# Choosing the experts of a PEER layer: a shorter list of candidates, one comparison a half, products on another engine

## The chip, the core and the metric

The kernel runs on one core of a Trainium2 chip. The metric is the device time of one execution in microseconds. TensorE (PE) multiplies matrices, VectorE (DVE), ScalarE (ACT) and GpSimd (POOL) work on tiles of 128 partitions, SyncE (SP) issues most of the transfers. Each engine takes its instructions in a fixed order and waits at an instruction until what it needs is there.

## The reference

The program is one decoder layer: two kinds of token mixing side by side, an output projection, and then a feed-forward layer of experts (PEER) for 512 tokens of width 2048. Only the choice of the experts changes. Cut to it, the reference is:

```python
q = (xb @ w_query).reshape(PEER_BLOCK, PEER_HEADS, 2, PEER_HALF)          # 8 heads, 2 halves of 128
s = jnp.einsum('lhpd,hpnd->lhpn', q, sub_keys)                            # 128 scores a half
s_half, i_half = lax.top_k(s, PEER_TOPK)                                  # the best 16 of each half
cand_s = s_half[:, :, 0, :, None] + s_half[:, :, 1, None, :]              # 16 x 16 sums
cand_i = i_half[:, :, 0, :, None] * PEER_N_KEYS + i_half[:, :, 1, None, :]
top_s, pos = lax.top_k(cand_s, PEER_TOPK)                                 # the best 16 sums
eidx = jnp.take_along_axis(cand_i, pos, axis=-1)                          # the experts' numbers
gates = jax.nn.softmax(top_s, axis=-1)
```

Each token so gets 16 of 16384 experts for each of 8 heads. Both lists of 16 are sorted, so the sum of place a in the first and place b in the second can be among the best 16 only if (a+1)(b+1) is at most 16. That holds for 50 pairs.

## The kernel before

The 512 tokens stand as four groups of 128 (`tt`). The stage around the change is the query stage, about 1378 to 1632 us of the span. It is a loop over 8 heads (`h`) and 2 halves (`hf`). For each half a projection `query` runs on TensorE: 16 steps over the width, each with six matmuls (three products of high and low parts, for the first 320 tokens and for the other 192), 96 in all, into a PSUM tile `mm`. The weights come in two pieces a half; `load_split` loads a piece `wr`, ScalarE casts it to its high part `whi`, GpSimd computes the low part `wlo` (helper `split`, lines 201 and 202). There are three `whi` and `wlo` buffers, so a split waits until TensorE has used the piece three before it. ScalarE copies the projection to `qT`, and four score products (L1039) write `sc`, of which there are two buffers. On VectorE follow, for each group of 128 tokens, two rounds of finding the best 8 of 128 with their places (L1043 to L1048).

After both halves of a head VectorE adds the sums into `cand`, 16 rows of 16 a token of which 50 places are used and the rest stays at a very small number (L1056, seven instructions), and finds the best 16 of the 256 places (L1063 to L1068). The position is taken apart into a row and a column (L1073 to L1077). For each half the index is fetched from the list `si` by comparing the place with 0 to 15, multiplying by the list and summing over 16 (`oh`, L1080 and L1082, four instructions each, one for each group of tokens; L1084). The softmax runs between them; its exponential `ex` is on ScalarE (L1088).

After the eighth head TensorE transposes the index tables `iall` and `jall` (L1108), VectorE makes the experts' numbers `ef`, `eu` and `eT`, and the stage of the experts begins: 192 of the tokens gather their own experts by indirect transfers from GpSimd's queue (L1252), and for the other 320 a dense pass over all experts runs on TensorE (`expert_u`, `expert_v`), masked by gates that `gate_block` builds. The first matmuls of that pass (of `expert_u`, also into `mm`) stand in TensorE's order already behind the last query and before the transposes. GpSimd computes `wlo` and `vlo` for the pass.

A scheduler sets each engine's order when the program is built, from the order of the code and its own estimate of durations. The order is fixed in the program. Buffers in a pool with `bufs=n` are used in turn.

## Time and profile before

| | us |
|---|---|
| median of 3 runs | 3998.52 (3996.01 to 4006.34) |
| the profiled execution | 4000.34 |
| its span, first to last instruction | 3998.3 |
| TensorE busy | 3671.5 (92%) |
| VectorE busy | 2473.4 (62%) |
| GpSimd busy | 2385.3 (60%) |
| ScalarE busy | 1455.9 (36%) |

Busy shares are means over stages with different limits. The stage of the change takes about 250 us of the span and is read from slices of its own. Where instructions of one engine follow each other closely, a row's length reaches a little into the next one's start, so the sum of lengths is larger than the time between the first and the last start. A merged row (x4) gives the time from the start of its first to the end of its last. A wait is put down to the event that came last.

### The profile page before, as it was taken

To read this page: it belongs to the slowest core of one execution; us is meant where nothing else is said; L and a number is where in the kernel's file an instruction comes from. 1 tells how busy PE (TensorE), PEld (TensorE's weight loads), DVE (VectorE), ACT (ScalarE), POOL (GpSimd) and SP (SyncE) were. 2 spreads that over 40 slices of the span, in tenths; PEclk is the share of its full clock that TensorE was granted. 3 is DMA by queue.
4 is the path that set the end of the run, shared out by engine and by line. 5 is a ranking of instruction groups with operands and counts; after the bars stand their busy time and mean duration, and the time that the engine had idled before them with its cause. 6 is when DMAs were issued, how large, how long until landed. Compare 5 with 4: busy or idle time off the path is not lost. (4 is left out here: it accounts for less than half of the span.)

```text
span 3998.3 us, 62039 instructions
## 1 busy us (share of the span) xinstructions
PE 3671.5 (92%) x23708; PEld 3046.1 (76%) x23708; DVE 2473.4 (62%) x4503; ACT 1455.9 (36%) x2548; POOL 2385.3 (60%) x1377
## 2 busy tenths in 40 slices
PE   5899999999999899688979999998999999999998
PEld 3667757666656799588858888887888888788888
DVE  7543145455641799898768787566756756674225
ACT  3434323343322411455643333333333333333333
POOL 5345434332413633566637788777878887787765
PEclk9999999998987999899979999999999999999999
DMA  8465662324252422687879988898999989889874
GB/s 338 168 206 176 212 175 72 84 73 132 80 188 79 137 66 77 239 321 281 309 262 338 343 334 331 317 329 317 333 327 344 331 316 328 317 333 337 297 274 127
DMA packets 314008, 964.35 MB, mean 241 GB/s; under 512 B 67376, under 2 KB 132656, under 8 KB 257584
## 3 DMA queue, kind: packets, MB, share of 16 engines
q1 hardware_dynamic: 258416, 557.72, 41.5%
q0 software_dynamic: 55296, 402.68, 26.6%
q8 instruction: 187, 3.06, 0.3%
q14 instruction: 109, 0.89, 0.1%
HBM read 914.34 MB, written 45.94 MB: 240 GB/s over the span
## 5 line engine op out<-in xcount | busy, mean ns | idle before, releaser
L202 POOL TENSOR_TENSOR wlo<-wr,whi 128x1024 fp32r<-128x1024 f32 (+3 forms) x544 | 1048.9, 1936 | 890.6 <-ACT whi L201 810.3
L202 POOL TENSOR_TENSOR vlo<-vr,vhi 128x1024 fp32r<-128x1024 f32 x256 | 633.2, 2482 | 265.9 <-ACT vhi L201 261.3
L207 PE MATMUL mm<-n2hi,wlo 128*128 128x320 f32 x2304 | 733.5, 319 | 39.0 <-POOL wlo L202 38.8
L205 PE MATMUL mm<-n2hi,whi 128*128 128x320 f32 x2304 | 732.5, 318 | 10.8 <-ACT whi L201 7.2
L206 PE MATMUL mm<-n2lo,whi 128*128 128x320 f32 x2304 | 722.4, 314 | 1.9 <-DVE n2lo L202 1.9
L1259 DVE SCALAR_TENSOR_TENSOR g<-g,row 128x1024 f32<-128x1024 f32 x384 | 708.4, 1881 | 3.3 <-DMA g<-in_u,eix 3.3
L201 ACT CAST whi<-wr 128x1024 fp32r<-128x1024 f32 (+3 forms) x544 | 454.3, 841 | 622.4 <-PE mm L206 309.1
L205 PE MATMUL po<-ghi,vhi 128*128 128x320 f32 x2048 | 641.3, 318 | 33.8 <-DVE hT L1224 20.7
L206 PE MATMUL po<-glo,vhi 128*128 128x320 f32 x2048 | 638.9, 314 | 10.4 <-DVE glo L202 10.0
L207 PE MATMUL po<-ghi,vlo 128*128 128x320 f32 x2048 | 616.3, 318 | 22.7 <-POOL vlo L202 22.3
L207 PEld LDWEIGHTS mm<-n2hi,wlo 128*128 128x128 f32 x2304 | 438.7, 190 | 99.4 <-POOL wlo L202 68.7
L205 PEld LDWEIGHTS mm<-n2hi,whi 128*128 128x128 f32 x2304 | 439.7, 191 | 36.4 <-issue 20.8
L205 PEld LDWEIGHTS po<-ghi,vhi 128*128 128x128 f32 x2048 | 391.4, 192 | 83.5 <-DVE hT L1224 24.0
L206 PEld LDWEIGHTS mm<-n2lo,whi 128*128 128x128 f32 x2304 | 439.6, 191 | 5.7 <-issue 3.4
L1184 DVE TENSOR_TENSOR act<-gd,act 128x320 f32<-128x320 f32 x128 | 179.1, 1409 | 418.9 <-ACT act L1158 396.9
L207 PEld LDWEIGHTS po<-ghi,vlo 128*128 128x128 f32 x2048 | 382.2, 192 | 72.0 <-POOL vlo L202 49.0
L1224 DVE SCALAR_TENSOR_TENSOR hT<-po,mod,hT 128x320 f32<-128x320 f32 x512 | 258.6, 544 | 244.3 <-PE po L207 235.2
L206 PEld LDWEIGHTS po<-glo,vhi 128*128 128x128 f32 x2048 | 393.1, 192 | 16.5 <-DVE glo L202 12.2
L201 ACT CAST vhi<-vr 128x1024 fp32r<-128x1024 f32 x256 | 267.8, 1048 | 277.9 <-PE po L206 130.0
L1252 POOL DMA_INDIRECT g<-in_u,eix x192 | 242.1, 1261 | 91.8 <-issue 47.2
L1252 POOL DMA_INDIRECT g<-in_v,eT x192 | 221.7, 1155 | 77.4 <-issue 29.5
L205 PE MATMUL mm<-nhi,whi 128*128 128x512 f32 x640 | 262.7, 410 | 4.5 <-ACT whi L201 4.5
(440 smaller groups left out, 5905.6 us busy)
## 6 DMA issues: line engine op xcount, KB each, us to landing
wr<-in_uT SPq DMA_DIRECT2D x256, 512.0 KB
vr<-in_vq SPq DMA_DIRECT2D x256, 512.0 KB
wr<-in_wrest SPq DMA_DIRECT2D x160, 256.0 KB
aw<-in_ada SPq DMA_DIRECT2D x32, 1024.0 KB
a2w<-in_adar SPq DMA_DIRECT2D x64, 512.0 KB
glD<-gb SPq DMA_DIRECT2D x10, 2048.0 KB
gd<-glD SPq DMA_DIRECT2D x32, 640.0 KB
a3w<-in_adar SPq DMA_DIRECT2D x32, 512.0 KB
```

What stands on the lines that cost most here:

```text
L201: copied.append(S.copy(hi, src))
L202: return (eng or V).tensor_tensor(lo, src, hi.bitcast(F32), OP.subtract)
L205: TE.matmul(ps, lhsT=whi, rhs=xhi, start=first, stop=False)
L206: TE.matmul(ps, lhsT=whi, rhs=xlo, start=False, stop=False)
L207: done_mm[0] = TE.matmul(ps, lhsT=wlo, rhs=xhi, start=False, stop=last)
L1184: V.tensor_tensor(a.rearrange("p (b t) -> p b t", t=TB), gd[:, :, i, :], a.rearrange("p (b t) -> p b t", t=TB), OP.mult)
L1224: V.scalar_tensor_tensor(h, po[d], mod2[:, 48 + k:49 + k], h, OP.mult, OP.add)
L1252: G.indirect_dma_start(out=g, out_offset=None, in_=I[s[0]], in_offset=bass.IndirectOffsetOnAxis(ap=ix, axis=0))
L1259: V.scalar_tensor_tensor(g[:, c], g[:, c], 1.0, n2s[i][:, c], OP.mult, OP.mult, accum_out=wtp[:, e, n:n + 1])
```

## The change

The 50 pairs now stand in ten rows of eight, 80 places a token: the first row holds the sums of place 0 with places 0 to 7 of the other half, the second place 0 with places 8 to 15, rows 2 to 8 the places 1 to 7 with as many as they need, and row 9 the sums of places 8 to 15 of the first half with place 0 of the second. The table has two buffers where it had one. The two rounds of search run over 80 columns. The position needs more steps to become two places (nine instructions on 64 columns in place of four). The comparison is one instruction a half for all four groups of tokens; the product with the index list is one instruction a half too, and moves to GpSimd; `oh` has two buffers. The sum over 16 stays on VectorE. Lines behind the change stand four further down (L1084 is now L1088, L1088 is L1092, L1108 is L1112).

```diff
--- before.py
+++ after.py
@@ -1018,8 +1018,10 @@
         gall = qp.tile([P, 4, P], F32, name="gall", bufs=1)
         iall = qp.tile([P, 4, P], F32, name="iall", bufs=1)
         jall = qp.tile([P, 4, P], F32, name="jall", bufs=1)
-        cand = [qp.tile([P, 4, 16, 16], F32, name="cand", bufs=1)] * 2
-        for t in cand[:1]:
+
+
+        cand = [qp.tile([P, 4, 10, 8], F32, name=f"cand{i}", bufs=1) for i in range(2)]
+        for t in cand:
             V.memset(t, -3.0e38)
         pss = [pu.tile([P, T], F32, name="mm", tag="mm") for _ in range(2)]
         query(pss, 0)
@@ -1049,38 +1051,40 @@
                 V.tensor_copy(si[:, hf], ix)
 
             cd = cand[h % 2]
-            a = 0
-            while a < 16:
-                nb = 16 // (a + 1)
-                e = max(x for x in range(a, 16) if 16 // (x + 1) == nb) + 1
-                V.tensor_tensor(cd[:, :, a:e, 0:nb], sv[:, 0, :, a:e].unsqueeze(3).to_broadcast([P, 4, e - a, nb]),
-                                sv[:, 1, :, 0:nb].unsqueeze(2).to_broadcast([P, 4, e - a, nb]), OP.add)
-                a = e
+            for r0, r1, a0, b0, nb in ((0, 1, 0, 0, 8), (1, 2, 0, 8, 8), (2, 3, 1, 0, 8), (3, 4, 2, 0, 5), (4, 5, 3, 0, 4),
+                                       (5, 6, 4, 0, 3), (6, 9, 5, 0, 2)):
+                V.tensor_tensor(cd[:, :, r0:r1, 0:nb],
+                                sv[:, 0, :, a0:a0 + r1 - r0].unsqueeze(3).to_broadcast([P, 4, r1 - r0, nb]),
+                                sv[:, 1, :, b0:b0 + nb].unsqueeze(2).to_broadcast([P, 4, r1 - r0, nb]), OP.add)
+            V.tensor_tensor(cd[:, :, 9, :], sv[:, 0, :, 8:16], sv[:, 1, :, 0:1].to_broadcast([P, 4, 8]), OP.add)
             tv = qp.tile([P, 4, 16], F32, name="tv")
             px = qp.tile([P, 4, 16], U32, name="px")
             for tt in range(4):
                 c2 = cd[:, tt].rearrange("p a b -> p (a b)")
                 V.max(tv[:, tt, 0:8], c2)
                 V.max_index(px[:, tt, 0:8], tv[:, tt, 0:8], c2)
-                s2_ = qp.tile([P, 256], F32, name="s3")
+                s2_ = qp.tile([P, 80], F32, name="s3")
                 V.match_replace(s2_, tv[:, tt, 0:8], c2, -3.0e38)
                 V.max(tv[:, tt, 8:16], s2_)
                 V.max_index(px[:, tt, 8:16], tv[:, tt, 8:16], s2_)
 
-            for hf, dst in ((0, iall), (1, jall)):
-                pi = qp.tile([P, 4, 16], U32, name="pi")
-                if hf == 0:
-                    V.tensor_scalar(pi, px, 4, None, OP.logical_shift_right)
-                else:
-                    V.tensor_scalar(pi, px, 15, None, OP.bitwise_and)
-                pf = qp.tile([P, 4, 16], F32, name="pf")
-                V.tensor_copy(pf, pi)
-                oh = qp.tile([P, 4, 16, 16], F32, name="oh", bufs=1)
-                for tt in range(4):
-                    V.tensor_tensor(oh[:, tt], pf[:, tt].unsqueeze(2).to_broadcast([P, 16, 16]),
-                                    iota16.unsqueeze(1).to_broadcast([P, 16, 16]), OP.is_equal)
-                    V.tensor_tensor(oh[:, tt], oh[:, tt], si[:, hf, tt].unsqueeze(1).to_broadcast([P, 16, 16]),
-                                    OP.mult)
+            pi = qp.tile([P, 4, 16], U32, name="pi")
+            row, c_ = (qp.tile([P, 4, 16], F32, name=n) for n in ("prow", "pcol"))
+            V.tensor_scalar(pi, px, 3, None, OP.logical_shift_right)
+            V.tensor_copy(row, pi)
+            V.scalar_tensor_tensor(c_, row, -8.0, px, OP.mult, OP.add)
+            ra, rb_ = (qp.tile([P, 4, 16], F32, name=n) for n in ("pa", "pb"))
+            V.scalar_tensor_tensor(ra, row, 9.0, c_, OP.is_equal, OP.mult)
+            V.tensor_tensor(rb_, c_, ra, OP.subtract)
+            V.tensor_scalar(c_, row, 1.0, 8.0, OP.is_equal, OP.mult)
+            V.tensor_tensor(rb_, rb_, c_, OP.add)
+            V.tensor_scalar(row, row, 1.0, -1.0, OP.max, OP.add)
+            V.tensor_tensor(ra, ra, row, OP.add)
+            for hf, r_, dst in ((0, ra, iall), (1, rb_, jall)):
+                oh = qp.tile([P, 4, 16, 16], F32, name="oh", bufs=2)
+                V.tensor_tensor(oh, r_.unsqueeze(3).to_broadcast([P, 4, 16, 16]),
+                                iota16.unsqueeze(1).unsqueeze(1).to_broadcast([P, 4, 16, 16]), OP.is_equal)
+                G.tensor_tensor(oh, oh, si[:, hf].unsqueeze(2).to_broadcast([P, 4, 16, 16]), OP.mult)
                 V.tensor_reduce(dst[:, :, 16 * h:16 * h + 16], oh, mybir.AxisListType.X, OP.add)
 
             ex = qp.tile([P, 4, 16], F32, name="ex")
```

The order moves at three places that matter. The first is GpSimd's queue in the middle of the stage. Before, there are only splits `wlo` of query pieces, four a head; the five rows here are the second piece of head 1, second half, both pieces of head 2, first half, and of head 2, second half:

```order
L202 TENSOR_TENSOR wlo_12340<-wr_12337,whi_12339 128x1024
L202 TENSOR_TENSOR wlo_12498<-wr_12495,whi_12497 128x1024
L202 TENSOR_TENSOR wlo_12552<-wr_12549,whi_12551 128x1024
L202 TENSOR_TENSOR wlo_12640<-wr_12637,whi_12639 128x1024
L202 TENSOR_TENSOR wlo_12694<-wr_12691,whi_12693 128x1024
```

After the change:

```order
L202 TENSOR_TENSOR wlo_12337<-wr_12334,whi_12336 128x1024
L202 TENSOR_TENSOR wlo_12490<-wr_12487,whi_12489 128x1024
L1087 TENSOR_TENSOR oh_12120<-oh_12120,si_12005 128x1024
L1087 TENSOR_TENSOR oh_12124<-oh_12124,si_12005 128x1024
L202 TENSOR_TENSOR wlo_12544<-wr_12541,whi_12543 128x1024
L202 TENSOR_TENSOR wlo_12632<-wr_12629,whi_12631 128x1024
L202 TENSOR_TENSOR wlo_12686<-wr_12683,whi_12685 128x1024
```

The two products of head 0 (`oh`) stand between the two pieces of the first half of head 2 (`wlo_12490` and `wlo_12544`), and so on for each head: the splits behind them wait with them.

The second place is VectorE's queue at the end of a head and the beginning of the next. Before, comparisons, products and sums of head 1 (`oh_12461`, `oh_12475`) are spread among the searches for head 2 (`sv_12492`):

```order
L1080 TENSOR_TENSOR oh_12461<-pf_12459,iota16_11777 128x256 x4
L1091 RECIPROCAL sm_12488<-sm_12488 128x4
L1044 MAX_INDEX ix_12610<-sv_12492,sc_12605 128x8
L1046 MATCH_REPLACE s2_12613<-sv_12492,sc_12605 128x128
L1043 MAX sv_12492<-sc_12605 128x8
L1082 TENSOR_TENSOR oh_12461<-oh_12461,si_12139 128x256 x4
L1092 TENSOR_TENSOR gall_11779<-ex_12485,sm_12488 128x4x16
L1047 MAX sv_12492<-s2_12613 128x8
L1044 MAX_INDEX ix_12610<-sv_12492,sc_12605 128x8
L1046 MATCH_REPLACE s2_12619<-sv_12492,sc_12605 128x128
L1043 MAX sv_12492<-sc_12605 128x8
L1084 TENSOR_REDUCE iall_11780<-oh_12461 128x4x16
```

After the change both comparisons of head 1 come first, and its first sum stands behind ten instructions of the next head's searches:

```order
L1085 TENSOR_TENSOR oh_12469<-pa_12461,iota16_11777 128x1024
L1085 TENSOR_TENSOR oh_12473<-pb_12462,iota16_11777 128x1024
L1045 MAX sv_12484<-sc_12597 128x8
L1046 MAX_INDEX ix_12602<-sv_12484,sc_12597 128x8
L1048 MATCH_REPLACE s2_12605<-sv_12484,sc_12597 128x128
L1045 MAX sv_12484<-sc_12597 128x8
L1049 MAX sv_12484<-s2_12605 128x8
L1046 MAX_INDEX ix_12602<-sv_12484,sc_12597 128x8
L1048 MATCH_REPLACE s2_12611<-sv_12484,sc_12597 128x128
L1045 MAX sv_12484<-sc_12597 128x8
L1050 MAX_INDEX ix_12602<-sv_12484,s2_12605 128x8
L1088 TENSOR_REDUCE iall_11780<-oh_12469 128x4x16
```

The second sum comes six rows further on. Both wait for GpSimd's products.

The third place is the end of the stage on ScalarE, from the copy of the last query to the copies of the transposed tables. Before, the exponential of the last head (`ex_14609`) stands behind all casts for the first experts:

```order
L1036 COPY qT_14515<-mm_14406 128x512
L201 CAST whi_16244<-wr_16242 128x1024
L201 CAST whi_16282<-wr_16280 128x1024
L201 CAST whi_16312<-wr_16310 128x1024
L201 CAST whi_16352<-wr_16350 128x1024
L1088 ACTIVATE ex_14609<-ex_14609 128x64
L1110 COPY iT_11487<-sc_14632 128x320
```

After the change it (`ex_14571`) stands before the last of them:

```order
L1038 COPY qT_14482<-mm_14373 128x512
L201 CAST whi_16206<-wr_16204 128x1024
L201 CAST whi_16244<-wr_16242 128x1024
L201 CAST whi_16274<-wr_16272 128x1024
L1092 ACTIVATE ex_14571<-ex_14571 128x64
L201 CAST whi_16314<-wr_16312 128x1024
L1114 COPY iT_11487<-sc_14594 128x320
```

On GpSimd the split of that last piece (`wlo_16315`) is followed by the two products of the last head:

```order
L202 TENSOR_TENSOR wlo_16207<-wr_16204,whi_16206 128x1024
L202 TENSOR_TENSOR wlo_16245<-wr_16242,whi_16244 128x1024
L202 TENSOR_TENSOR wlo_16275<-wr_16272,whi_16274 128x1024
L202 TENSOR_TENSOR wlo_16315<-wr_16312,whi_16314 128x1024
L1087 TENSOR_TENSOR oh_14563<-oh_14563,si_14230 128x1024
L1087 TENSOR_TENSOR oh_14567<-oh_14567,si_14230 128x1024
L1128 IOTA iota_14633 128x128
L1256 DMA g_16164<-in_u,eix_11495 128x2048
```

So the last products now stand behind a split whose cast waits for the exponential. On TensorE the order inside the stage is the same as before: 32 matmuls of the following half stand ahead of each four score products, and 66 matmuls of the first two experts between the last scores and the transposes. In the stage of the experts GpSimd's order is the same but for four places, and TensorE's differs in places where the scheduler interleaves two streams of matmuls.

## Rows read from the trace of the kernel before

**Rows 1.** Windows: stretch, length, busy of PE, PEld, DVE, ACT, POOL; clock, DMA

```profile
1400.00:1420.00 20.00, 20.00 (x158) 20.00 (x157) 19.90 (x77) 4.13 (x5) 7.40 (x3) 1.00 0.25 80
...
1480.00:1500.00 20.00, 17.34 (x124) 17.07 (x123) 19.90 (x85) 2.62 (x4) 4.85 (x2) 0.91 0.15 47
...
1600.00:1620.00 20.00, 4.38 (x30) 4.11 (x29) 19.86 (x95) 2.10 (x2) 5.89 (x4) 0.73 0.24 79
```

**Rows 2.** Waits, 1379 to 1634 us: who for whom, total us, times, longest

```profile
POOL wlo L202 <- ACT whi L201: 149.6, 26, 15.3
...
ACT ex L1088 <- DVE ex L1087: 112.1, 8, 16.6
...
PE sc L1108 <- DVE iall L1084: 22.1, 1, 22.1
```

**Rows 3.** PE in order of time (start us, length us, engine, line, operation)

```profile
1396.52 1.05 PE L1039 MATMUL sc<-skT,qT 128*128 128x128 f32 x8
...
1436.42 1.05 PE L1039 MATMUL sc<-skT,qT 128*128 128x128 f32 x8
...
1592.13 1.91 PE L1039 MATMUL sc<-skT,qT 128*128 128x128 f32 x8
...
1604.07 0.31 PE L207 MATMUL mm<-n2hi,wlo 128*128 128x320 f32 x1
```

**Rows 4.** POOL in order of time, two heads

```profile
1463.88 4.85 POOL L202 TENSOR_TENSOR wlo<-wr,whi 128x1024 fp32r<-128x1024 f32 x2 [14.70 <-ACT whi L201]
...
1471.16 2.39 POOL L202 TENSOR_TENSOR wlo<-wr,whi 128x1024 fp32r<-128x1024 f32 x1 [2.42 <-ACT whi L201]
...
1495.01 4.85 POOL L202 TENSOR_TENSOR wlo<-wr,whi 128x1024 fp32r<-128x1024 f32 x2 [15.25 <-ACT whi L201]
```

**Rows 5.** DVE in order of time, the last head

```profile
1608.52 0.30 DVE L1043 MAX8 sv<-sc 128x8 f32<-128x128 f32 x1
...
1614.33 1.41 DVE L1063 MAX8 tv<-cand 128x8 f32<-128x256 f32 x4
...
1629.31 1.22 DVE L1084 TENSOR_REDUCE jall<-oh 128x64 f32<-128x1024 f32 x1
```

**Rows 6.** DVE in order of time, one head in the middle

```profile
1455.01 1.41 DVE L1063 MAX8 tv<-cand 128x8 f32<-128x256 f32 x4
...
1462.36 0.22 DVE L1087 TENSOR_TENSOR ex<-tv 128x64 f32<-128x64 f32 x1
...
1462.49 0.20 DVE L1073 TENSOR_SCALAR pi<-px 128x64 uint32<-128x64 uint32 x1
...
1462.60 0.19 DVE L1075 TENSOR_SCALAR pi<-px 128x64 uint32<-128x64 uint32 x1
...
1463.27 5.75 DVE L1080 TENSOR_TENSOR oh<-pf,iota 128x256 f32<-128x256 f32 x4
...
1469.75 1.41 DVE L1082 TENSOR_TENSOR oh<-oh,si 128x256 f32<-128x256 f32 x4
...
1472.15 1.20 DVE L1084 TENSOR_REDUCE iall<-oh 128x64 f32<-128x1024 f32 x1
```

**Rows 7.** Groups by form on DVE, 1379 to 1632 us: busy us, mean ns

```profile
L1044 DVE FIND_INDEX8 ix<-sv,sc 128x8 uint32<-128x128 f32 x64 | 18.5, 289 | 0.0
...
L1064 DVE FIND_INDEX8 px<-tv,cand 128x8 uint32<-128x256 f32 x32 | 13.2, 420 | 0.0
```

**Rows 8.** Groups by form on POOL, whole span

```profile
L699 POOL TENSOR_TENSOR BK<-BK,WL 128x1024 f32<-128x1024 f32 x8 | 15.2, 1897 | 39.1 <-PE bd L667 39.1
...
L655 POOL TENSOR_TENSOR BK<-kr,t 64x512 f32<-64x512 f32 x8 | 12.0, 1501 | 0.5
```

**Rows 9.** ACT in order of time, the last cast of the stage

```profile
1604.31 1.04 ACT L201 CAST whi<-wr 128x1024 fp32r<-128x1024 f32 x1 [2.47 <-PE mm L206]
```

**Rows 10.** Windows behind the stage

```profile
1660.00:2000.00 340.00, 299.52 (x2002) 281.35 (x2003) 292.13 (x362) 201.61 (x401) 215.09 (x109) 0.97 0.83 307
...
2080.00:3000.00 920.00, 867.21 (x5677) 763.47 (x5678) 642.15 (x748) 297.71 (x396) 714.42 (x375) 0.98 0.90 329
```

## The prediction, made before the changed kernel ran

> **What bounds the kernel now.** I read the span in slices first, then the waits of the slices that stood out, then the engines' rows in order of time inside them. The change touches one stage only, the query stage from about 1378 to 1632 us. In its slices VectorE is busy in every microsecond (19.9 of 20 and 19.86 of 20), TensorE is full only at the start (20.00 of 20 at 1400) and falls to 17.34 at 1480 and 4.38 at 1600, GpSimd is busy 4.85 to 7.40 of 20 us [rows 1]. The waits give the direction: ScalarE waited 112.1 us for the `ex` of VectorE, GpSimd 149.6 us for casts that stand behind those on ScalarE, and TensorE at last 22.1 us for the index sums [rows 2]. So VectorE sets the pace, through ScalarE's queue, and the stage ends when VectorE's last index sum is there.
>
> What TensorE would do alone is in its own rows: the score products of successive halves start at 1396.52 and 1436.42, three halves apart, 13.3 us each, 26.6 us a head [rows 3]. What VectorE imposes is in GpSimd's rows: the pair of splits that opens a head recurs at 1463.88 and 1495.01, 31.13 us a head [rows 4]. The last score products start at 1592.13, TensorE runs dry at 1604.07 + 0.31 [rows 3] and then has those 22.1 us without work, and the last index sum ends at 1629.31 + 1.22 = 1630.53 [rows 5].
>
> **VectorE's 31.13 us, part by part.** Neighbours overlap by about 0.09 us (one of 0.20 us at 1462.49, the next at 1462.60 [rows 6]), so I count from start to start.
>
> - Choice among the candidates: 1455.01 to 1462.36 is 7.35 us [rows 6], 20 searches of 256 columns and their loads. A search of 256 columns takes 420 ns, of 128 columns 289 [rows 7]: 1.02 ns a column. No row shows 80 columns. By that slope it is 240 ns, and 20 x 0.18 = 3.6 us go; if it were no shorter than 128 columns, 20 x 0.13 = 2.6 us go. I take 3.5, since the slope holds between two measured widths.
> - Products: four of 256 columns take 1.41 us, 1.33 to the next start [rows 6]; two such groups leave VectorE, 2.66 us.
> - Comparisons: one of 1024 columns instead of four of 256. The sum over 1024 columns takes 1.20 us [rows 6], 1.11 to its successor by that overlap; I take 1.12 against 1.33, twice 0.21 = 0.4 us saved (nothing, if the broadcast of four dimensions costs more).
> - Decoding the position: nine instructions of 64 columns for four. At 0.11 us each [rows 6] that adds 0.55; but they form a chain, and if each waited for the end of the one before (0.20 and a handover) it would add 1.8. I take 1.2; three other instructions of the softmax stand between them in the order. One more addition into the candidates: 0.1.
> - The stall: the same group of four comparisons takes 5.75 us at 1463.27 [rows 6], while GpSimd does two splits, 4.85 us from 1463.88 [rows 4]. The excess is 4.34 us. A sum over 1024 columns at 1472.15 keeps its 1.20 us although a split runs from 1471.16 [rows 4]. So instructions with two operands in SBUF stand still while GpSimd works, searches and sums don't. Whether such stalls remain depends on the phase of the two engines; I leave it out of the sum here and weigh it below.
>
> Without any stall: 31.13 - 4.34 - 3.5 - 2.66 - 0.4 + 1.2 + 0.1 = 21.5 us a head. TensorE needs 26.6. So VectorE has 5.1 us a head for stalls before it is the bound again, and my forecast is that TensorE becomes the bound of the stage.
>
> **What the products do on GpSimd.** 16 of 128x1024. No row shows this shape with an inner run of 16. A product of 128x1024 with a broadcast took 1.90 us, one of 64x512 with split rows 1.50 on the mean, so 3.0 for 1024 [rows 8]; I take 2.2. They add 4.4 to four splits of 2.4 us a head, 14 of 26.6 us. The Trainium skill, "GPSIMD Engine Reference", section "4.1 Engine selection", speaks against the move: two-operand elementwise work belongs on VectorE, GpSimd being about twice as slow. By its 4497 ns for 2048 columns the estimate is 2.25 us; what the row of 1.90 adds is that GpSimd has the room here.
>
> The queue decides whether they harm. In GpSimd's order the products of head k stand behind the first split of head k+2 and before its second, and behind them wait that split and three more. Measured from the second scores of head k: VectorE has its four searches and sums of candidates after 6 us, the choice after 10, decoding after 11.5, both comparisons after 14; with one stall of 2.4 us, 16.4. The products end at 21, the second split of head k+2 at 23.4. TensorE first does the rest of the half it is in (64 of 96 matmuls, 8 us), the next half (13.3) and half of the following one (6): it needs that split at 27 to 28. Some 4 us are left, so TensorE doesn't wait. The sums stand about ten and sixteen searches further on in VectorE's order; they may wait for a product there, 1 to 3 us a head, in time that VectorE has free.
>
> **The end of the stage.** TensorE-bound, the last scores start 13 halves after 1396.52: 1396.5 + 13 x 13.3 = 1569.4, against 1592.13 (the last step holds 30 matmuls of the first expert for 32 of a half, which I count alike). From there VectorE, no longer behind, needs 0.5 for the scores, 5.8 for the last four searches and the candidates (1608.52 to 1614.33 [rows 5]) and 3.9 for the choice: `ex` at 10.2. Now ScalarE's last cast stands behind `ex`, and GpSimd's last split behind that cast, before the products: a cast of 1.04 [rows 9] and a split of 2.4, with the handovers done at 14. VectorE's decoding and comparisons fall under that split; the first comparison ends at about 15.5, the second at 17. The two products end at 21.5, the last sum at 22.7: 1592.1 instead of 1630.5. That is 38 us, 22.7 from the pace and the rest from VectorE no longer being a head half behind when the last scores come.
>
> **What stands behind the stage.** TensorE's order there holds the same expert matmuls in the same sequence but for a few places, GpSimd's the same gathers. TensorE is busy 299.5 of 340 us and 867 of 920 [rows 10]; the rest is waits on data whose loads hang on the same instructions, so I let the whole stage shift: no part of the gain is given back, and none added. The memset of two tiles of 320 columns for one of 1024 stands in VectorE's order before the stage and only gets shorter; I give it nothing.
>
> **Sum.** The profiled execution took 4000.34 us (span 3998.3 and 2.0 around it); 4000.3 - 38.4 = 3961.9. The median of the runs is 1.8 lower, so 3960.
>
> **Rivals.**
>
> 1. VectorE stays the bound (0.20). For: the stall of 4.34 us a head is there today, and the products give GpSimd 4.4 us more in which VectorE's 8 additions, decoding and comparisons stand still. Against: they come when VectorE has gone on to searches. If the stall stays whole and 2.5 us come on top, a head takes 28.3 instead of 31.1: 8 x 2.8 = 22 us, less 4 for the last products that nothing covers: 18 us, 3981. If still 2 us more are lost a head, 2 us are left, which is no change. The Trainium skill, "SBUF — State Buffer", section "Who interferes with whom", gives the rule (an exclusive lock for the whole instruction, a VectorE instruction with two SBUF inputs against a GpSimd one that reads). The trace agrees: 5.75 against 1.41 us under the splits.
> 2. Slower (0.04): products so slow that they hold the splits. Slack of 4 us at 2.2 us a product is used up at 4.3; beyond, each us costs two a head in the seven heads that feed splits, 14 us. From 7 us a product on all the gain is gone, at 8 the time is 4012. Nothing in GpSimd's rows for tensors of this size comes near that [rows 8].
> 3. The stage gains, and the expert stage takes part of it back (0.09): its loads start when TensorE is at another place of the stream, and 40 of 340 us there are waits [rows 10]. Half of the gain lost: 3979.
>
> **Chances.** Forecast 0.67, the three rivals 0.20, 0.04 and 0.09. What can be told from no change is 0.3%, 12 us: below 3986.5 is faster, above 4010.5 slower. The forecast and rival 3 are faster, of rival 1 three quarters; of rival 2 three quarters are slower, and the rest of both is no change: faster 0.91, same 0.06, slower 0.03. The forecast's own range is 3950 to 3970 (products 1.9 to 3.0 us, decoding 0.55 to 1.8, a phase of the last split). The range reaches down to 3945, for a tail without the last stall and some us gained behind the stage, and up to 3983 to hold the likelier part of rivals 1 and 3.
>
> **What would show it.** After the change the score products should stand 13.3 us apart to the end, the last at about 1570; TensorE full to there; VectorE below 95% in the middle of the stage; searches of 80 columns at about 240 ns; products on GpSimd near 2.2 us; the last index sum ending near 1592. I am wrong if the scores still stand more than 14 us apart (then a look at whether VectorE is full or TensorE waits for a split tells rival 1 from 2), or if the last sum is at 1592 and the end has not moved by the same 38 us.

## The result and the profile after

The changed kernel took 3950.6 us (median of 4 runs, 3944.97 to 3963.35), the kernel before 3999.4 in the same series (4 runs): ratio 0.988, interval 0.9853 to 0.9908. Run again in another series it took 3956.6 (3951.96 to 3962.92) against 4002.3: 0.9895, 0.9874 to 0.9916. The profiled execution took 3952.57 us (span 3950.6) where the one of before took 4000.34.

The slices of the stage that answer to [rows 1]:

```profile
1400.00:1420.00 20.00, 20.00 (x159) 20.00 (x158) 18.68 (x99) 4.37 (x6) 9.04 (x4) 1.00 0.33 105
1480.00:1500.00 20.00, 20.00 (x158) 20.00 (x158) 18.55 (x99) 4.38 (x6) 8.94 (x4) 1.00 0.32 106
...
1580.00:1600.00 20.00, 7.38 (x30) 6.58 (x31) 11.32 (x20) 5.51 (x13) 9.29 (x5) 0.52 0.31 78
```

TensorE is now full in the middle of the stage at a granted clock of 1.00 (17.34 of 20 us at 0.91 before), and VectorE isn't any more (18.55 against 19.90). Two waits of before that [rows 2] doesn't show, then the waits of the stage after the change:

```profile
ACT whi L201 <- PE mm L206: 53.0, 11, 6.5
...
PE sc L1039 <- ACT qT L1036: 10.3, 4, 2.9
```

```profile
ACT whi L201 <- PE mm L206: 107.1, 24, 6.3
POOL wlo L202 <- ACT whi L201: 66.4, 18, 5.3
...
POOL oh L1087 <- DVE oh L1085: 25.7, 8, 3.6
ACT ex L1092 <- DVE ex L1091: 21.2, 8, 6.5
...
PE sc L1112 <- DVE iall L1088: 13.9, 1, 13.9
```

The direction has turned round. ScalarE's casts wait for TensorE to give a buffer back, 107 us instead of 53; its wait for VectorE's `ex` fell from 112 to 21 us, and TensorE's for `qT`, which stood behind `ex` in ScalarE's queue, is gone. Only the last wait, TensorE's for the index sums, is still there, 13.9 instead of 22.1 us. TensorE in order of time, for [rows 3]:

```profile
1390.87 1.05 PE L1041 MATMUL sc<-skT,qT 128*128 128x128 f32 x8
...
1430.89 1.05 PE L1041 MATMUL sc<-skT,qT 128*128 128x128 f32 x8
...
1564.51 1.05 PE L1041 MATMUL sc<-skT,qT 128*128 128x128 f32 x8
...
1574.94 0.31 PE L207 MATMUL mm<-n2hi,wlo 128*128 128x320 f32 x1
1589.17 1.11 PE L1112 MATMUL sc<-ident,iall 128*128 128x128 f32 x4 [13.92 <-DVE iall L1088]
```

From the first of these to the last scores 13 halves take 173.64 us, 13.36 each, without a gap up to the end. The whole stage, from the second head's first scores to the end of the last index sum, as one window; first before, then after:

```profile
1396.52:1630.53 234.01, 195.51 (x1430) 193.27 (x1428) 232.98 (x954) 39.06 (x53) 73.85 (x31) 0.91 0.22 71
```

```profile
1390.87:1591.41 200.54, 185.49 (x1430) 184.83 (x1428) 186.32 (x875) 40.13 (x52) 116.75 (x47) 0.97 0.26 83
```

The same 1430 matmul records; 33.5 us fewer. TensorE's time without work fell from 38.5 to 15.1 us, which is 23.4, and its busy time by 10.0, while the granted clock of the stretch rose from 0.91 to 0.97. Before, TensorE did some of its matmuls behind a wait at the lower of its two levels (1.2 and 2.4 GHz). One of the four waits for `qT`:

```profile
1465.29 1.76 PE L1039 MATMUL sc<-skT,qT 128*128 128x128 f32 x8 [2.10 <-ACT qT L1036]
```

Without such a wait these eight matmuls take 1.05 us; from 1466 to 1469 us the granted clock was 0.50. The end of the program moved by 47.7 us in this pair. The other 14.2 lie outside the stage: it began 5.6 us earlier, and from the last index sum to the end it is 2359.2 us against 2367.8.

### The profile page after: what moved, and what is told of

It reads as the page before. It is cut to its first block, busy times and chain, and to the rows that moved or that the text cites. A ratio compares the mean times of both kernels' runs of the same rounds, so it can differ in the third digit from the quotient of the medians.

```text
span 3950.6 us, 61998 instructions
## 1 busy us (share of the span) xinstructions
PE 3647.2 (92%) x23708; PEld 3033.3 (77%) x23708; DVE 2431.9 (62%) x4440; ACT 1454.1 (37%) x2548; POOL 2429.3 (61%) x1393
## 3 DMA queue, kind: packets, MB, share of 16 engines
q0 software_dynamic: 55296, 402.68, 26.8%
## 4 chain that ended last, share of the span: by engine, by line
PE 66%; DVE 11%; POOL 7%; DMA 6%; issue 5%; ACT 1%; SPq 0%; POOLq 0%; DVEq 0%; ACTq 0%
PE mm L207 12%; PE mm L205 12%; PE mm L206 11%; PE po L207 6%; PE po L205 5%; PE po L206 5%; DVE g L1263 4%; PE pw L1277 3%; POOL vlo L202 3%; POOL wlo L202 2%; POOL g L1256 2%; DVE I L1146 2%; DMA AI<-abD 1%; PE pg L1151 1%; DVE act L1188 1%
## 5 line engine op out<-in xcount | busy, mean ns | idle before, releaser
L1263 DVE SCALAR_TENSOR_TENSOR g<-g,row 128x1024 f32<-128x1024 f32 x384 | 732.3, 1943 | 7.0 <-DMA g<-in_u,eix 3.9
```

The source lines that it names most:

```text
L1263: V.scalar_tensor_tensor(g[:, c], g[:, c], 1.0, n2s[i][:, c], OP.mult, OP.mult, accum_out=wtp[:, e, n:n + 1])
```

## The experiments

Pace is the time of a head (two halves) from the eighth to the fourteenth scores of the stage; stage is the stretch of the window above; rest is the time from its end to the end of the span; these three come from one profiled execution each. A ratio is that to runs of the kernel before in the same series. VectorE's own work a head is counted without stalls: 31.13 - 4.34 = 26.8 for the kernel before, and from there with the start-to-start times measured in the changed kernel (choice 3.69 instead of 7.35, decoding 1.70 instead of 0.44, a comparison of 1024 columns 1.14 instead of 1.33, one more addition 0.1; the products 2.66 where they leave; the softmax 0.47 where it leaves).

| kernel | median us (runs) | ratio, interval | own work | pace | stage | rest |
|---|---|---|---|---|---|---|
| before | 3999.4 (4) | | 26.8 | 31.1 | 234.0 | 2367.8 |
| before again | 3997.5 (10) | 0.9999, 0.9984 to 1.0015 | 26.8 | 31.1 | 234.2 | 2375.1 |
| after | 3950.6 (4) | 0.988, 0.9853 to 0.9908 | 21.5 | 26.7 | 200.5 | 2359.2 |
| after again | 3956.6 (4) | 0.9895, 0.9874 to 0.9916 | 21.5 | 26.7 | 200.5 | 2360.0 |
| list only | 3956.7 (4) | 0.988, 0.9855 to 0.9905 | 24.5 | 26.7 | 200.6 | 2366.4 |
| operations only | 3956.4 (4) | 0.9884, 0.985 to 0.9919 | 23.8 | 26.6 | 200.1 | 2360.7 |
| products on VectorE | 3954.2 (4) | 0.9892, 0.9869 to 0.9914 | 23.7 | 26.7 | 199.4 | 2362.0 |
| products twice | 3969.3 (5) | 0.9926, 0.9903 to 0.995 | 21.5 | 26.7 | 211.7 | 2364.4 |
| fewer matmuls | 3929.1 (4) | 0.982, 0.9788 to 0.9851 | 21.5 | 23.3 | 178.9 | 2364.2 |
| one softmax | 3995.1 (10) | 0.9987, 0.9971 to 1.0003 | 26.3 | 30.5 | 232.4 | 2366.6 |
| one comparison | 3985.3 (6) | 0.9957, 0.994 to 0.9974 | 26.4 | 31.5 | 235.1 | 2354.9 |
| one comparison, again | 3987.3 (12) | 0.997, 0.9953 to 0.9986 | 26.4 | 30.5 | 231.1 | 2361.8 |
| both small edits | 3982.7 (10) | 0.9956, 0.9938 to 0.9974 | 25.9 | 30.4 | 231.5 | 2363.6 |

**The changed kernel once more**, beside the first three experiments, and the kernel before as a kernel of its own, beside the next two, to see the scatter.

> The changed kernel once more, on the chip of the next three kernels. Both theories: scores 13.3 us apart, last index sum near 1591 us, time 3945 to 3963. If the 8 us that the stage doesn't explain (the end moved by 47.7, the last index sum by 39.1 us) belong to the order behind the stage, the stretch from the last sum to the end is again near 2359 us; if they are scatter of executions, it lies anywhere between 2355 and 2370.

> The kernel before once more with a profile. Open is why the end moved by 47.7 us where the stage itself, from the second head's first scores to the last index sum, got only 33.5 us shorter (234.0 to 200.5). If the rest is scatter of executions, the first scores of the second head move by several us from 1396.5 here, and the stretch from the last sum to the end from 2367.8. If it belongs to the order that the scheduler gave the kernel, both are again within 2 us of these.

Both stages came out to 0.2 us as they had been (200.5 and 234.2), so the 33.5 us are no scatter. What lies outside is less firm: the rest of the changed kernel was 2359.2 and 2360.0, as if it belonged to the order; that of the kernel before was 2367.8 and 2375.1, and its second head's first scores came at 1396.5 and 1392.7, as scatter would have it.

**The list alone**: the kernel before with the ten rows of eight, the shorter searches and the new decoding; comparisons and products in four of 256 columns on VectorE. Beside the lines of the change above the comparison, only the name of the place in it differs from before:

```diff
-                    V.tensor_tensor(oh[:, tt], pf[:, tt].unsqueeze(2).to_broadcast([P, 16, 16]),
+                    V.tensor_tensor(oh[:, tt], r_[:, tt].unsqueeze(2).to_broadcast([P, 16, 16]),
...
```

> The short list of candidates and its decoding, but comparisons and products as before: four of 256 columns each a half, all on VectorE. Theory (a change of bound with a cap: VectorE's work a head falls from 31.1 us until TensorE's 26.7 takes over): VectorE's work without stalls is 21.5 + 2.7 + 0.4 = 24.6 us a head, with the stalls of the kernel before 26.7 to 28.9, so the pace is 26.7 to 28.5 us a head, the last index sum ends at 1595 to 1612, the time is 3955 to 3978. Rival (each part gives its own share of VectorE's time, 3.5 - 1.3 of 9.6 us a head and so a quarter of the gain): about 12 us, time near 3988.

The stage took 200.6 us: this half of the change alone brings the whole gain of the stage, as the theory had it and not the rival of shares. Its comparisons and products are the same instructions as before. Their groups by form between 1400 and 1560 us (busy us, mean ns of one), first of the kernel before, then of this one:

```profile
L1080 DVE TENSOR_TENSOR oh<-pf,iota 128x256 f32<-128x256 f32 x44 | 36.9, 899 | 0.0
L1082 DVE TENSOR_TENSOR oh<-oh,si 128x256 f32<-128x256 f32 x40 | 17.7, 500 | 0.0
...
L1056 DVE TENSOR_TENSOR cand<-sv 128x32 f32<-128x32 f32 x10 | 1.9, 189 | 0.0
```

```profile
L1056 DVE TENSOR_TENSOR cand<-sv 128x32 f32<-128x32 f32 x18 | 11.3, 655 | 0.0
L1086 DVE TENSOR_TENSOR oh<-pb,iota 128x256 f32<-128x256 f32 x24 | 9.4, 448 | 0.0
L1086 DVE TENSOR_TENSOR oh<-pa,iota 128x256 f32<-128x256 f32 x24 | 8.6, 420 | 0.2
```

A comparison takes 420 to 448 ns instead of 899: the stall has left it. It stands now at the additions into the candidates (655 ns for 32 columns, 189 before).

**The operations alone**: the list of 256 as before, one comparison of 1024 columns a half, and the products as one instruction on GpSimd.

```diff
-                oh = qp.tile([P, 4, 16, 16], F32, name="oh", bufs=1)
-                for tt in range(4):
...
+                oh = qp.tile([P, 4, 16, 16], F32, name="oh", bufs=2)
+                V.tensor_tensor(oh, pf.unsqueeze(3).to_broadcast([P, 4, 16, 16]),
...
+                G.tensor_tensor(oh, oh, si[:, hf].unsqueeze(2).to_broadcast([P, 4, 16, 16]), OP.mult)
```

> One comparison a half and the products on GpSimd, but the list of 16 rows of 16 and its decoding as before. Theory (change of bound with a cap): VectorE without stalls 31.1 - 4.3 - 2.7 - 0.4 = 23.7 us a head, stalls of 3 to 4 us as in the changed kernel, so 26.7 to 27.7 a head; the last head is 3.5 us longer; last index sum at 1595 to 1606, time 3955 to 3970. Together with the list alone the two gains add up to clearly more than the gain of both at once. Rival (shares): three quarters of the gain, 36 us, time near 3963, and the two gains add up to that of the whole change.

200.1 us, again the whole gain of the stage. The 3.5 us that the longer search was expected to cost in the last head didn't show: from the last scores to the end of the last sum it was 26.95 us, as after the change (26.90). The two halves of the change don't add: either takes VectorE's own work below TensorE's 26.7 us a head, and from there nothing more is to be had in this stage. In both kernels VectorE is all but full beside a full TensorE (list only: 79.1 of the 80.0 us from the eighth to the fourteenth scores); one slice of this one:

```profile
1480.00:1500.00 20.00, 20.00 (x159) 20.00 (x159) 19.86 (x101) 3.97 (x7) 9.65 (x5) 1.00 0.32 106
```

VectorE's 23.8 us of own work and its stalls together fill 26.6. So the stalls take 2.8 us a head here where they took 4.3 before: they aren't a fixed price.

**The products back on VectorE**, one instruction of 1024 columns a half; all else as after the change.

```diff
-                G.tensor_tensor(oh, oh, si[:, hf].unsqueeze(2).to_broadcast([P, 4, 16, 16]), OP.mult)
+                V.tensor_tensor(oh, oh, si[:, hf].unsqueeze(2).to_broadcast([P, 4, 16, 16]), OP.mult)
```

> The changed kernel with the products on VectorE (one instruction of 1024 columns a half). Theory: VectorE has room for them, 25.5 us a head with stalls now, 2.2 more for the products, 1.5 less because GpSimd holds it up less: 26 to 26.7, so TensorE still sets the pace of 26.7, and the last index sum ends between 1588 and 1593; time as the changed kernel within 4 us. Rival (taking the products off VectorE is what made TensorE the bound): pace 27.5 or more, last index sum at 1598 or later, time 8 us or more above the changed kernel.

The stage took 199.4 us, the median 3954.2: with the short list, the move to GpSimd brings nothing that the rest of the change hadn't brought. With the long list it seems to decide: one comparison a half with the products on VectorE (below) left the stage at 231 to 235 us, the operations with the products on GpSimd took it to 200.1; but these two kernels also differ in the number of product instructions and of `oh` buffers.

**The products twice**: a second product of the same shape (by ones) ahead of each on GpSimd.

```diff
+                G.tensor_tensor(oh, oh, ones[:, 0:16].unsqueeze(1).unsqueeze(1).to_broadcast([P, 4, 16, 16]), OP.mult)
                 G.tensor_tensor(oh, oh, si[:, hf].unsqueeze(2).to_broadcast([P, 4, 16, 16]), OP.mult)
```

> The changed kernel with every product on GpSimd done after one more of the same size (a multiplication by one), so 2.8 us more for each half, 5.7 a head. It prices the slack in GpSimd's queue. Theory: the second split behind the products comes 0.3 to 1 us too late for TensorE, and VectorE, which waits for the products inside its searches, has little room left: 25.5 us of 26.7 a head are its own work and stalls. Pace 28 to 31 us a head, last index sum 15 to 40 us later than in the changed kernel counted from the first scores of the second head (200.5 us there), time 3970 to 3995. Rival (GpSimd is busy 60% of the stage, so there is room for 5.7 of 26.7 us): pace stays 26.7, only the last head is longer, 5 to 6 us.

The scores kept their 13.3 us a half up to 1530.7, then came 13.9 and 20.1 us: the stage was 11.1 us longer. GpSimd at the beginning of the products of two earlier heads and at the last two heads (start us, length us), then the longest of TensorE's waits for a split:

```profile
1413.96 5.65 POOL L1087 TENSOR_TENSOR oh<-oh,ones 128x1024 f32<-128x1024 f32 x2 [3.85 <-DVE oh L1085]
...
1440.92 5.67 POOL L1087 TENSOR_TENSOR oh<-oh,ones 128x1024 f32<-128x1024 f32 x2 [4.12 <-DVE oh L1085]
...
1553.15 5.66 POOL L1087 TENSOR_TENSOR oh<-oh,ones 128x1024 f32<-128x1024 f32 x2 [9.08 <-DVE oh L1085]
1558.77 2.34 POOL L1088 TENSOR_TENSOR oh<-oh,si 128x1024 f32<-128x1024 f32 x1
1561.07 2.34 POOL L202 TENSOR_TENSOR wlo<-wr,whi 128x1024 fp32r<-128x1024 f32 x1
...
1584.27 5.55 POOL L1087 TENSOR_TENSOR oh<-oh,ones 128x1024 f32<-128x1024 f32 x2 [1.78 <-DVE oh L1085]
1589.78 4.64 POOL L1088 TENSOR_TENSOR oh<-oh,si 128x1024 f32<-128x1024 f32 x2
```

```profile
1563.46 0.64 PE L207 MATMUL mm<-n2hi,wlo 128*128 128x320 f32 x1 [5.70 <-POOL wlo L202]
```

So the queue that rival 2 of the prediction spoke of is real. A pair of products takes 10.2 to 10.4 us in place of 5.7, and that is already a little too much: from 1413.96 to 1440.92 a head took GpSimd 26.96 us where TensorE needs 26.68. TensorE kept its pace while it still had split pieces ahead, and waited 5.7 us for one when that lead was used up. Of the 11.1 us, 7.1 come from the scores of the last two halves and 4.1 from the tail, where the products stand without cover. The rival of this expectation had the pace of the first heads; in a longer loop the theory's slower pace would be what one sees, but no run here is longer.

**Fewer matmuls**: 15 of the 96 matmuls of a half aren't issued.

```diff
-                        mm3(ps[:, TD:T], whi[:, i, :], wlo[:, i, :], ngh[k], ngl[k], False, k == KT - 1)
+                        if k == KT - 1:
+                            mm3(ps[:, TD:T], whi[:, i, :], wlo[:, i, :], ngh[k], ngl[k], False, True)
+                        else:
+                            TE.matmul(ps[:, TD:T], lhsT=whi[:, i, :], rhs=ngh[k], start=False, stop=False)
+                            TE.matmul(ps[:, TD:T], lhsT=whi[:, i, :], rhs=ngl[k], start=False, stop=False)
```

> The changed kernel without 15 of the 16 third products (low part of the weights) for the 192 gathered tokens in every query half; this part of the computation is left out. TensorE needs 15 x 0.11 = 1.65 us less a half, 3.3 a head, 23.4 us. Theory (TensorE is the bound of the stage now, VectorE is 1 to 1.5 us a head behind it): the pace falls at once, but only to 25 to 25.7 us a head, and the stretch from the second head's first scores to the last index sum from 200.5 to 189 to 195 us. Rival 1 (VectorE or GpSimd is the bound already and TensorE only looks full): no change, 199 to 201. Rival 2 (VectorE has much room): the whole 14 x 1.65, 178 us.

The pace followed TensorE: 11.67 us a half, 23.3 a head, 178.9 us for the stage. One slice:

```profile
1480.00:1500.00 20.00, 20.00 (x154) 20.00 (x153) 19.60 (x105) 4.85 (x6) 14.93 (x6) 1.00 0.27 80
```

So TensorE is the bound after the change, and VectorE, with 21.5 us of own work, lets it go to 23.3. That is rival 2 of the expectation; its theory (25 to 25.7) failed by counting VectorE's stalls as work that stays.

**One softmax behind the loop.** By now it had seemed that the stall of before was self-made: ScalarE's casts queue behind `ex`, which VectorE delivers late, and so two splits come together [rows 4] when VectorE compares. Without `ex` in the loop they can't.

```diff
-            tv = qp.tile([P, 4, 16], F32, name="tv")
+            tv = tvall[:, h]
...
-            ex = qp.tile([P, 4, 16], F32, name="ex")
-            V.tensor_tensor(ex, tv, tv[:, :, 0:1].to_broadcast([P, 4, 16]), OP.subtract)
-            S.activation(ex, ex, AF.Exp)
...
+        V.tensor_tensor(exall, tvall, tvall[:, :, :, 0:1].to_broadcast([P, 8, 4, 16]), OP.subtract)
+        S.activation(exall, exall, AF.Exp)
...
```

> The kernel before, with one softmax for all eight heads behind the loop, so that ScalarE has no `ex` between its casts; candidates, choice, comparisons and products as before. Theory: the stall of 4.34 us a head is self-made: casts queue behind an `ex` that VectorE delivers late, and so two casts and two splits come as a pair just when VectorE compares. Without `ex` in the loop the splits come singly as TensorE delivers; VectorE loses some 0.45 us of work a head and most of the stall, 31.1 - 4.3 - 0.45 = 26.3, so TensorE's 26.7 is about the bound: 26.7 to 28.5 a head, from the second head's first scores to the last index sum 201 to 218 us against 234, in all 3965 to 3982. Rival 1: the stall has nothing to do with `ex`, splits and comparisons meet anyway: 30.7 a head, 231 us, 3994 to 3998. Rival 2: the casts are released as early as before, but the stall moves to the candidate sums and costs half: 28.5 to 30, 218 to 227 us, 3982 to 3992.

GpSimd in order of time, three splits in the middle of the stage:

```profile
1480.57 2.50 POOL L202 TENSOR_TENSOR wlo<-wr,whi 128x1024 fp32r<-128x1024 f32 x1 [10.06 <-ACT whi L201]
1486.76 2.40 POOL L202 TENSOR_TENSOR wlo<-wr,whi 128x1024 fp32r<-128x1024 f32 x1 [3.69 <-ACT whi L201]
1493.86 2.69 POOL L202 TENSOR_TENSOR wlo<-wr,whi 128x1024 fp32r<-128x1024 f32 x1 [4.70 <-ACT whi L201]
```

VectorE's groups by form, 1400 to 1560 us:

```profile
L1084 DVE TENSOR_TENSOR oh<-oh,si 128x256 f32<-128x256 f32 x40 | 22.0, 609 | 0.0
L1082 DVE TENSOR_TENSOR oh<-pf,iota 128x256 f32<-128x256 f32 x40 | 19.7, 553 | 0.0
...
L1058 DVE TENSOR_TENSOR cand<-sv 128x32 f32<-128x32 f32 x10 | 5.9, 585 | 0.0
```

The splits came singly, six to seven us apart, as meant, and the pace stayed at 30.5: the stall went from the comparisons (899 to 553 ns) to the products (500 to 609) and to the additions (189 to 585). The theory of the self-made stall falls. Rival 1 of that expectation had the pace and the time; that the stall would move stood in rival 2, but it didn't shrink by it.

**One comparison a half**, all else as before the change.

```diff
+                V.tensor_tensor(oh, pf.unsqueeze(3).to_broadcast([P, 4, 16, 16]),
+                                iota16.unsqueeze(1).unsqueeze(1).to_broadcast([P, 4, 16, 16]), OP.is_equal)
                 for tt in range(4):
-                    V.tensor_tensor(oh[:, tt], pf[:, tt].unsqueeze(2).to_broadcast([P, 16, 16]),
-                                    iota16.unsqueeze(1).to_broadcast([P, 16, 16]), OP.is_equal)
```

> The kernel before, with one comparison of 1024 columns a half in place of four of 256, the products in four of 256 on VectorE as before; `ex` where it was. VectorE's work falls by 0.4 us a head only. Theory of the self-made stall: casts and splits still come as a pair behind `ex` at the comparisons, and one long comparison stands still as four do: 30 to 31 a head, 225 to 234 us from the second head's first scores to the last index sum, 3988 to 3999. Rival: the meeting is a matter of phase that any small saving undoes (31.1 - 0.4 - 4.3 = 26.4, so TensorE's 26.7 would bind): 201 to 210 us, 3963 to 3975.

Its two groups on VectorE:

```profile
L1082 DVE TENSOR_TENSOR oh<-oh,si 128x256 f32<-128x256 f32 x40 | 35.5, 946 | 0.0
L1079 DVE TENSOR_TENSOR oh<-pf,iota 128x1024 f32<-128x1024 f32 x11 | 17.4, 1583 | 0.0
```

The stall moved once more, to the products (500 to 946 ns), and the stage kept its length, 235.1 us. The time fell by 16 us nevertheless, below the theory's range and without the rival's shorter stage; so the kernel ran again:

> The kernel with one comparison a half once more, unchanged: it had 16 us less than before although its stage took 235 us against 234. If that lies in the program, the ratio is again 0.994 to 0.997 and the time behind the last index sum again 8 to 15 us under that of before; if it was the scatter of one series, the ratio is 0.998 to 1.001 and that time is 2362 to 2372 us, as in the other profiled runs.

11.5 us less than before, the ratio (0.997) as in the first case; the stage 231.1, the rest 2361.8, at the edge of the second. So some of it seems to lie in the program and outside the stage; a part of it is found below.

**Both small edits together**, to see how much room the stalls need.

> The kernel before with both small edits, one softmax behind the loop and one comparison of 1024 columns a half. Without stalls VectorE needs 31.1 - 4.3 - 0.45 - 0.4 = 25.9 us a head, 0.8 under TensorE's 26.7. Theory: once VectorE is the bound the stalls are 4.3 to 4.9 us a head wherever the splits fall (each small edit alone left 30.5 to 31 a head), and 0.8 of room isn't enough: 30.0 to 30.8 a head, 224 to 231 us from the second head's first scores to the last index sum, 3978 to 3992. Rival: the stalls give way as soon as VectorE's own work is below TensorE's, and TensorE's pace is kept: 201 to 208 us, 3955 to 3970.

231.5 us and a pace of 30.4: 0.8 us of room isn't enough, as the theory had it. With 24.5 us of own work or less (list only) TensorE's pace is kept, with 25.9 or more it isn't. These kernels so fall in two groups by their own work, and the point lies between; that own work alone decides, and not also where the splits fall in the loop, is not shown.

## Why the prediction was right, and where it wasn't

The forecast was 3960 us, with a range of 3945 to 3983; the two series gave 3950.6 and 3956.6.

**The bound and the pace** were right. VectorE set the pace, and after the change TensorE does, at 26.7 us a head against 26.6 predicted.

**VectorE's 21.5 us** were right in the sum and nearly in the parts. The groups by form after the change, over the stage (busy us, mean ns):

```profile
L1051 DVE CAST si<-ix 128x64 f32<-128x64 uint32 x16 | 15.0, 940 | 0.2
...
L1085 DVE TENSOR_TENSOR oh<-pb,iota 128x1024 f32<-128x1024 f32 x8 | 9.8, 1219 | 0.0
L1065 DVE FIND_INDEX8 px<-tv,cand 128x8 uint32<-128x80 f32 x32 | 7.3, 236 | 0.0
L1068 DVE MAX8 tv<-s 128x8 f32<-128x80 f32 x32 | 6.0, 228 | 0.0
```

A search of 80 columns takes 228 to 236 ns (240 predicted from the slope), a comparison of 1024 columns 1.22 (1.20), and decoding cost 1.26 more (1.2).

**The stalls** were left out of the sum as something that depends on the phase, and that held, but they didn't go: 26.7 less 21.5, less 1.2 us of waiting for scores, leaves some 4 us a head after the change too, against 4.34 before. They went to other instructions, and they fall into time that VectorE has free. In one head (subtraction for `ex`, cast, two additions; undisturbed about 0.2, 0.2 and 0.3 us):

```profile
1443.01 0.74 DVE L1091 TENSOR_TENSOR ex<-tv 128x64 f32<-128x64 f32 x1
...
1455.59 1.90 DVE L1051 CAST si<-ix 128x64 f32<-128x64 uint32 x1
...
1462.57 1.71 DVE L1056 TENSOR_TENSOR cand<-sv 128x32 f32<-128x32 f32 x2
```

The prediction held that only instructions with two operands in SBUF stand still. The cast of `si`, which has one, does too: 940 ns in the mean, where undisturbed ones take about 200, and the one at 1455.59 ends with the pair of splits that ends at 1457.44 (below). The Trainium skill, "SBUF — State Buffer", section "Who interferes with whom", has it: a cast can also take the pair of ports that GpSimd uses. The trace agrees by the 940 ns in the mean.

**The products on GpSimd** were mis-sized. GpSimd in the middle of the stage, and at its end:

```profile
1447.07 5.65 POOL L1087 TENSOR_TENSOR oh<-oh,si 128x1024 f32<-128x1024 f32 x2 [3.40 <-DVE oh L1085]
1452.68 4.76 POOL L202 TENSOR_TENSOR wlo<-wr,whi 128x1024 fp32r<-128x1024 f32 x2
...
1580.48 2.34 POOL L202 TENSOR_TENSOR wlo<-wr,whi 128x1024 fp32r<-128x1024 f32 x1 [5.28 <-ACT whi L201]
1584.60 5.56 POOL L1087 TENSOR_TENSOR oh<-oh,si 128x1024 f32<-128x1024 f32 x2 [1.78 <-DVE oh L1085]
```

Their lengths one by one (shortest, median, longest in ns):

```profile
L1087 POOL TENSOR_TENSOR oh<-oh,si x16: 2342/2828/3316, 1393.9 to 1587.8; 128x1024 f32<-128x1024 f32 x16
```

A pair takes 5.65 us, not 4.4. The second of a pair takes 2.34; the first starts as VectorE begins its second comparison (1.22 us) and needs 3.3. The 1.25 us more lie inside the 4 us of room that the prediction counted. That TensorE didn't wait for splits is shown by its full slices; the doubled products, 4.7 us more a pair, went a little beyond the room.

**The last scores** came at 1564.5, not at 1569.4: the stage began 5.6 us earlier in this execution, and 13 halves took 173.6 us where 172.9 had been counted. **The tail** took 26.9 us from the last scores to the end of the last sum, not 22.7. VectorE there:

```profile
1569.50 2.33 DVE L1056 TENSOR_TENSOR cand<-sv 128x32 f32<-128x32 f32 x2
...
1573.33 1.92 DVE L1056 TENSOR_TENSOR cand<-sv 128x32 f32<-128x32 f32 x1
...
1580.65 2.25 DVE L1080 TENSOR_TENSOR pb<-pb,pcol 128x64 f32<-128x64 f32 x1
...
1590.19 1.22 DVE L1088 TENSOR_REDUCE jall<-oh 128x64 f32<-128x1024 f32 x1 [1.08 <-POOL oh L1087]
```

The whole difference is there before `ex`. It came 14.5 us after the last scores, not 10.2, mainly because two stalls at the candidates (2.33 us for two additions and 1.92 for one, where one undisturbed takes 0.17) were not counted. From `ex` to the end of the last sum it was 12.4 us, 12.5 predicted: the decoding stood still under the last split (2.25 us, from 1580.65 to the end of that split), but the prediction let the first comparison end 1.5 us behind that split anyway (1.7 measured); and the longer pair of products began under the second comparison and not behind it. The last sum ended at 1591.4 against 1592.1 predicted. That it came so near is luck: a start 5.6 us early and a tail 4.2 us long nearly cancelled.

**"No part of the gain is given back, and none added"** is the step that failed. The prediction had 38.4 us, all from the stage. The stage brought 33.5, counted from the same scores, and the medians fell by 46 to 49. So the stage gave 5 us less than counted and what lies outside it gave 12 to 15 more; that these two partly cancelled is luck. It is the second sign of being wrong that the prediction named: the last sum near 1592, and the end moved by 47.7 us and not by 38. Rival 3, that the expert stage takes a part back, went the other way round.

Part of the difference is scatter: the start of the stage lay between 1384.0 and 1398.6 in the thirteen profiled executions though nearly all before it is the same, and the rest between 2354.9 and 2375.1. But every kernel with an edit had a rest of 2354.9 to 2366.6 us, and the kernel before, in its two executions, 2367.8 and 2375.1. By the medians 5 to 17 us (gain less what the stage brought, by kernel) come from outside the stage.

The traces of the stretch behind the last index sum say a little more. TensorE's 14442 matmul records there are the same in all kernels (14443 in one). Its time without work (the length of that stretch less TensorE's busy time in it) repeats when a kernel runs again: 176.2 and 176.4 us for the kernel before, 174.7 and 173.9 after the change, 168.5 and 168.2 with one comparison a half. So 8 us of what that kernel gained is less waiting behind the stage, and belongs to its program; of what the changed kernel gained outside, only 2. What remains is in TensorE's busy time, which doesn't repeat: 2191.5 and 2198.7 us before, 2184.5 and 2186.0 after the change, 2186.4 and 2193.6 with one comparison. Whether that is scatter or has a cause in the change, no run here isolates.

Rivals 1 and 2 didn't come about. Rival 1 had the right mechanism for the kernels whose own work is 25.9 us or more: there the stalls do hold VectorE at 30.4 to 31.5 us.

## What to carry to other kernels

Where two engines run at nearly the same pace, count each one's work without its stalls and compare those; a stall by contention isn't a price of the instruction that shows it. In this case, taking work away beside it only moved the stall until the engine had some us of room a turn (2.2 of 26.7 were enough, 0.8 weren't), and then the pace jumped to that of the other engine at once and gained nothing further. So one of two edits may be enough: here the shorter list, or the operations, each alone brought all that the stage had to give.

## What the runs showed of the hardware

- The stall moves with the phase. Where VectorE sets the pace, its sum (pace less own work) is 4.1 to 5.1 us a head: 4.34 at the comparisons before; spread over additions, comparisons and products with single splits (pace 30.5); at the products with one comparison (946 against 500 ns). Where TensorE sets the pace it varies: 2.8 with the operations alone, at most 2.2 with the list alone, some 4 after the change.
- Contention works both ways: a GpSimd product of 128x1024 takes 2.34 us alone and 3.3 when it begins while a comparison of VectorE (1.22 us) runs.
- Waiting costs TensorE twice: in the stage, 23.4 us less without work came with 10.0 us less busy time for the same matmul records, the granted clock going from 0.91 to 0.97; behind a wait of 2.10 us, eight matmuls took 1.76 us in place of 1.05.
- Over the 59 runs of the kernel before that stood beside the experiments, a granted clock higher by 0.001 goes with 2.0 us less (least squares). So a part of the scatter between runs goes with the clock; what moves the clock from run to run is not shown.
